# Moving 12 modulation chunks of a diffusion trunk's first stage from TensorE to VectorE

## The chip, the cores and the metric

One Trainium2 chip, one of its cores. The time is the device time of one execution in microseconds (us): lower is better. Before: 2353.95 us, the median of 3 runs (2353.66 to 2355.96). The engines are called PE (TensorE, the matmuls), DVE (VectorE), ACT (ScalarE), POOL (GpSimd) and SP (SyncE, whose queue issues the loads).

## The reference: what is computed

One step of a two-layer trunk (width D = 2048) over 128 context tokens `xp` and 128 latent tokens `xs`, all in fp32. Each layer is an attention half and an MLP half, and each half is scaled, shifted and gated by six vectors of 2048 that are made from a conditioning vector: `c_ctx` for the context tokens, `c` for the latent ones.

```python
def modulation(cvec, w_ada_l, b_ada_l):
    m = jax.nn.silu(cvec) @ w_ada_l + b_ada_l
    return jnp.split(m[:, None, :], N_MOD, axis=-1)
...
sh_a, sc_a, gt_a, sh_m, sc_m, gt_m = modulation(c, w_ada[l], b_ada[l])
h = rms_norm(xs, g_pre_a) * (1.0 + sc_a) + sh_a
...
o = mix_latent(h, ctx, w_in[l], w_out[l], na_rpb[l], gqa_q_g[l], gqa_k_g[l], ...)
xs = xs + gt_a * rms_norm(o, g_post_a)
h = rms_norm(xs, g_pre_m) * (1.0 + sc_m) + sh_m
xs = xs + gt_m * rms_norm(squared_relu_mlp(h, w_up[l], w_down[l]), g_post_m)
```

The context tokens go the same way with `c_ctx`. The attention has three kinds of heads side by side, one with a learned bias `na_rpb` by relative position, and small parameters for each layer (`qg`, `kg`, `dg`, `lam`). `w_ada` (2048 x 12288 for each layer) is as much work to load as the other weights, but is multiplied by two vectors only.

## The kernel before, in words

Every weight is read from HBM once, in chunks of 1 MB (128 x 2048 fp32) into one of `NRAW` = 5 buffers `raw`. The list `items` holds the order of the work, built by hand for each stage, and `issue` (L988) sends the loads on SP's queue in the order of that list, a new one when a buffer is released. There are four kinds of items.

- *Trunk chunk* ("t"). It is taken in two halves. For each, ACT rounds `raw` to `wh` (L1001) and DVE makes the remainder `wl` = `raw` - `wh` (L1002); 3 buffers of each, so that the split runs up to two halves ahead. PE multiplies a chunk by 24 products of 128 x 512 (L349 to L351: high by high, high by low, low by high) or, in the MLP's first product, by 48 of 128 x 256 (L384 to L386). In the first stage the sums of a segment are added up by DVE in `stg` (L782).
- *Modulation chunk on PE* ("ada", `ada_mm`, L140). 8 matmul records against the silu of the two conditioning vectors in `sT`. After four chunks (a block: 512 of the 2048 outputs of one of the six vectors) ACT copies the sum to `pt` (L144), PE transposes it (L111), DVE reduces it (L157), and `mod_fin` (L174, L175, L177) or `gate_fin` finishes it.
- *Modulation chunk on DVE* ("dv", `dv_mul`, L195). The transposed weights `w_adaT` are multiplied by `sB`, the silu of a conditioning vector copied to all partitions, and summed along the row: one multiply of 128 x 2048 into `junk` for the context tokens, and one into `raw` itself for the latent tokens, behind which the buffer is released. Up to two such chunks wait in `dvq`; each half of a trunk chunk moves the queue by half a step, or by a whole one while two wait. `sB` comes from two 1 MB loads and two activations (`load_sb`, L185, L187).
- *Call*: code that runs at that point of the list, such as `layer_consts` (L675 to L700). It loads `qg`, `kg`, `dg` into `bcs`, then `lam`, then the bias table `rpb` into `cv`; writes the table to DRAM (`rpbz`, L692); and reads it back in four pieces with other strides (`biasB`, L698). SP waits for the landing of each of the last three before it sends the next. DVE's and ACT's part is L676 to L686 and L700.

`weave` spreads modulation chunks among trunk chunks. The list says in which order the program is written; a scheduler with a cost model then sets each engine's order, so an operation can stand somewhat before or behind its place in the list.

The first stage of layer 0 is the start, a first quarter of the features (t0 to t7 and the modulation that it needs), feature quarters 2 to 4 (`f` = 1 to 3, t8 to t31), the rest of the input projection (`c2`, t32 to t35), and the output projection (`rest`, t36 to t51). Attention runs in between. Modulation is in blocks: M_A (shift and scale of the attention half), G_A (its gate), M_M and G_M (the same for the MLP). Of this stage 80 chunks are on PE, 8 in the first quarter as half-width pieces. The stage ends with `after_attn`: `use` runs four more modulation chunks that were loaded early into the `XT` buffers, `drain_dv` and `drain_fast` finish what is pending, `residual` (L309 to L321) makes the new `x`, with four L314 for each kind of token, and `make_xt` (L248 to L267) normalises and transposes it for the MLP. In the MLP's list of layer 0, 64 dv chunks are woven among the trunk chunks.

## Time and profile before

| what | value |
| --- | --- |
| median of 3 runs | 2353.95 us |
| the profiled execution, own time | 2356.2 us |
| its span in the profile | 2354.4 us |
| granted clock of PE, mean | 0.99 |
| PE busy | 2281.3 us (97%) |
| DVE busy | 1613.0 us (69%) |
| ACT busy | 1101.0 us (47%) |
| chain that ended last | PE 87%, DVE 5%, DMA 3%, ACT 2%, issue 2% |

The profiled execution is 2.25 us above the median, and its span leaves out 1.8 us around it. The shares are means over stages with different limits: the first stage (to about 490 us) carries attention and most of the modulation on PE, the MLP of layer 0 carries dv chunks on DVE.

### The profile page before, as it was taken

Reading aid. Unit: us, or ns where it says so; the run is one execution under the profiler, and the core shown is the slowest. Engines: PE = TensorE matmul, PEld = TensorE weight load, DVE = VectorE, ACT = ScalarE, POOL = GpSimd, SP = SyncE. Lnnn points to the kernel's source line nnn. Section 1 sums busy time; section 2 is a strip of 40 time slices with the busy share of each in tenths; the row PEclk is TensorE's granted clock in tenths of the full one; section 3 lists DMA queues with packets and bytes.
Section 4 is the critical chain, followed back from the end, with each engine's and each line's share of the span. In section 5 each row is a group of like instructions: output and inputs, shape, how many; then the busy total and the mean of one; then the engine's idle time right before and its main releaser. Section 6 shows DMA issues by size and latency. Waiting matters only on the chain.

```text
span 2354.4 us, 33079 instructions
## 1 busy us (share of the span) xinstructions
PE 2281.3 (97%) x13480; PEld 1905.2 (81%) x13480; DVE 1613.0 (69%) x2028; ACT 1101.0 (47%) x1525; POOL 25.6 (1%) x30
## 2 busy tenths in 40 slices
PE   6999999989999999999998999999999999999998
PEld 3567666669889889889867777877989988988986
DVE  2566755479888998999767787647666566565545
ACT  4334444464444445435445455546444444543543
POOL 0000000000000000000000000000000000000000
PEclk9999999999999999999999999999999999999999
DMA  8888787878877778777845766675666566565552
GB/s 323 305 328 336 274 321 302 332 249 303 308 269 292 292 293 294 279 286 286 337 179 197 270 223 233 226 268 200 228 217 219 211 221 222 201 219 212 191 183 90
DMA packets 92496, 601.35 MB, mean 255 GB/s; under 512 B 13752, under 2 KB 16184, under 8 KB 21432
## 3 DMA queue, kind: packets, MB, share of 16 engines
q1 hardware_dynamic: 91624, 598.64, 68.9%
q8 instruction: 105, 1.72, 0.3%
q10 hardware_dynamic: 720, 0.61, 0.1%
q14 instruction: 47, 0.39, 0.0%
HBM read 591.61 MB, written 7.60 MB: 255 GB/s over the span
## 4 chain that ended last, share of the span: by engine, by line
PE 87%; DVE 5%; DMA 3%; ACT 2%; issue 2%; POOL 1%; SPq 0%; ACTq 0%; POOLq 0%; DVEq 0%
PE acc L349 16%; PE acc L350 16%; PE acc L351 16%; PE acc L386 10%; PE acc L385 10%; PE acc L384 10%; PE ada L140 3%; PE m L111 2%; DVE wl L1002 2%; DMA raw<-w_adaT_in 2%; PE m L472 1%; POOL st L108 1%; PE m L223 1%; DVE raw L195 1%; DVE junk L195 0%
## 5 line engine op out<-in xcount | busy, mean ns | idle before, releaser
L1001 ACT ACTIVATE wh<-raw 128x1024 fp32r<-128x1024 f32 x720 | 759.0, 1059 | 924.0 <-PE acc L351 542.9
L1002 DVE TENSOR_TENSOR wl<-raw,wh 128x1024 fp32r<-128x1024 f32 x720 | 875.0, 1223 | 430.3 <-ACT wh L1001 427.7
L386 PE MATMUL acc<-XT,wl 128*128 128x256 f32 x2048 | 580.9, 284 | 1.6 <-DVE wl L1002 1.4
L385 PE MATMUL acc<-XT,wh 128*128 128x256 f32 x2048 | 580.1, 283 | 0.3 <-DVE XT L267 0.3
L384 PE MATMUL acc<-XT,wh 128*128 128x256 f32 x2048 | 577.6, 282 | 2.8 <-ACT XT L266 2.8
L349 PE MATMUL acc<-wh,big 128*128 128x512 f32 x1280 | 502.2, 395 | 0.0
L350 PE MATMUL acc<-wl,big 128*128 128x512 f32 x1280 | 499.9, 391 | 1.7 <-DVE wl L1002 1.7
L351 PE MATMUL acc<-wh,big 128*128 128x512 f32 x1280 | 498.2, 390 | 0.0
L384 PEld LDWEIGHTS acc<-XT,wh 128*128 128x128 f32 x2048 | 388.1, 190 | 4.3 <-ACT XT L266 3.5
L386 PEld LDWEIGHTS acc<-XT,wl 128*128 128x128 f32 x2048 | 387.5, 189 | 2.8 <-DVE wl L1002 2.6
L385 PEld LDWEIGHTS acc<-XT,wh 128*128 128x128 f32 x2048 | 386.8, 189 | 1.1 <-DVE XT L267 0.8
L349 PEld LDWEIGHTS acc<-wh,big 128*128 128x128 f32 x1280 | 239.9, 188 | 63.9 <-issue 11.0
L350 PEld LDWEIGHTS acc<-wl,big 128*128 128x128 f32 x1280 | 240.4, 188 | 52.0 <-DVE wl L1002 3.5
L351 PEld LDWEIGHTS acc<-wh,big 128*128 128x128 f32 x1280 | 240.3, 188 | 50.3
L349 PE MATMUL acc<-wh,XT 128*128 128x512 f32 x576 | 231.0, 411 | 6.8 <-ACT wh L1001 4.0
L195 DVE SCALAR_TENSOR_TENSOR junk<-raw,sB 128x2048 fp8e5<-128x2048 f32 x92 | 210.5, 2288 | 33.1 <-DMA raw<-w_adaT_in 32.7
L350 PE MATMUL acc<-wl,XT 128*128 128x512 f32 x576 | 230.4, 400 | 2.4 <-DVE wl L1002 2.3
L351 PE MATMUL acc<-wh,XT 128*128 128x512 f32 x576 | 228.4, 397 | 0.0
L195 DVE SCALAR_TENSOR_TENSOR raw<-raw,sB 128x2048 f32<-128x2048 f32 x92 | 210.3, 2286 | 0.0
L349 PEld LDWEIGHTS acc<-wh,XT 128*128 128x128 f32 x576 | 108.6, 190 | 48.7 <-ACT wh L1001 11.3
L350 PEld LDWEIGHTS acc<-wl,XT 128*128 128x128 f32 x576 | 109.3, 190 | 32.3 <-DVE wl L1002 7.5
L351 PEld LDWEIGHTS acc<-wh,XT 128*128 128x128 f32 x576 | 109.0, 189 | 24.6 <-issue 0.2
(134 smaller groups left out, 1235.6 us busy)
## 6 DMA issues: line engine op xcount, KB each, us to landing
raw<-w_up_in SPq DMA_DIRECT2D x128, 1024.0 KB, 5.2
raw<-w_down_in SPq DMA_DIRECT2D x128, 1024.0 KB, 5.0
raw<-w_adaT_in SPq DMA_DIRECT2D x92, 1024.0 KB, 4.9
raw<-w_ada_in SPq DMA_DIRECT2D x80, 1024.0 KB, 6.3
raw<-w_in_in SPq DMA_DIRECT2D x72, 1024.0 KB, 5.6
raw<-w_out_in SPq DMA_DIRECT2D x32, 1024.0 KB, 4.9
XT<-w_ada_in SPq DMA_DIRECT2D x12, 1024.0 KB, 7.6
raw<-w_ada_in SPq DMA_DIRECT2D x16, 512.0 KB, 5.1
```

The source lines that it names most:

```text
L108: pool.tensor_tensor(out, out, hf[:, 0:width], ALU.pow)
L111: pe.transpose(out, in_, ident)
L140: pe.matmul(pa[32 * g:32 * g + 32, 0:w], sT[:, 4 * kq + g, :], raw[:, g * w:(g + 1) * w], start=(kq == 0), stop=(kq == 3), tile_position=( ...
L195: dve.scalar_tensor_tensor(o, raw, 1.0, sB[v], ALU.mult, ALU.mult, accum_out=a[:, j, v:v + 1], saturate=None if v else False)
L349: pe.matmul(a, xh, wh[:, c], start=first, stop=False)
L350: pe.matmul(a, xh, wl[:, c], start=False, stop=False)
L351: pe.matmul(a, xl, wh[:, c], start=False, stop=last)
L384: pe.matmul(a, wh[:, c], xh, start=first, stop=False)
L385: pe.matmul(a, wh[:, c], xl, start=False, stop=False)
L386: pe.matmul(a, wl[:, c], xh, start=False, stop=last)
L1001: act.activation(wh, r, AF.Copy)
L1002: dve.tensor_tensor(wl, r, wh.bitcast(F32), ALU.subtract)
```

## The change

Three blocks of layer 0, twelve chunks, go from "ada" to "dv": G_A[0], G_A[1] and the last of M_M. Three of them are woven into the second feature quarter, three into the third, two into the fourth, and four are handed to the output projection's list. The fill on PE shrinks from 48 to 36 chunks: 8 in the fourth quarter as before, 4 instead of 8 in `c2`, and the rest in the output projection. `load_sb` moves from the MLP's list to just before `layer_consts`. The MLP's 64 dv chunks are spread over 116 entries of its list instead of 115, from one earlier on.

```diff
--- before.py
+++ after.py
@@ -34,8 +34,8 @@
 G_A, G_M = [(2, b) for b in range(4)], [(5, b) for b in range(4)]
 M_A = [(i, f) for f in range(4) for i in range(2)]
 M_M = [(3 + i, f) for f in range(4) for i in range(2)]
-DV_BLOCKS = [G_M, M_A + M_M[:4] + G_A[:3] + G_M]
-PE_BLOCKS = [M_A[2:] + G_A + M_M, M_M[4:] + G_A[3:]]
+DV_BLOCKS = [G_A[:2] + M_M[7:] + G_M, M_A + M_M[:4] + G_A[:3] + G_M]
+PE_BLOCKS = [M_A[2:] + G_A[2:] + M_M[:7], M_M[4:] + G_A[3:]]

@@ -812,7 +812,7 @@
         c2 = tchunks(wi, 32, 4, g2, k4)
         if l == 0:
             items.insert(0, ("call", startup))
-            fill, dv = ada_items(0, G_A + M_M), []
+            fill, dv = ada_items(0, G_A[2:] + M_M[:7]), dv_items(0, G_A[:2] + M_M[7:])
             h0 = lambda h: [("ada", I["w_ada0"][sec, h, kq], (0, sec, 0, kq, h)) for sec in range(2) for kq in range(4)]
             items.extend(h0(0)[:2])
             call(pre_norm_first)
@@ -826,19 +826,22 @@
             items.extend(a1[:2] + m[3:4] + a1[2:4] + m[4:5] + a1[4:6] + m[5:6] + a1[6:] + m[6:7])
             xt(1)
             items.extend(m[7:])
+            call(load_sb)
             for f in range(1, 4):
                 ch = [c for cg in cG for c in cg[2 * f:2 * f + 2]]
                 if f == 1:
                     call(lambda l=l: layer_consts(l))
                 if f < 3:
-                    weave(ch[:5], ada_items(0, M_A[2 * f + 2:2 * f + 4]))
+                    weave(ch[:5], ada_items(0, M_A[2 * f + 2:2 * f + 4]), dv[:3])
+                    dv = dv[3:]
                     items.append(ch[5])
                     xt(f + 1)
                     items.extend(ch[6:])
                 else:
-                    weave(ch, fill[:8])
-            weave(c2, fill[8:16])
-            rest, fill = [], fill[16:]
+                    weave(ch, fill[:8], dv[:2])
+                    dv = dv[2:]
+            weave(c2, fill[8:12])
+            rest, fill = [], fill[12:]
         else:
             for f in range(4):
                 call(lambda f=f: make_xt(1, 0, f))
@@ -877,11 +880,14 @@
             rest += tchunks(I["w_out"][l], 8 * nh, 8, Group(2, KT, o_lhs(), wout_done(nh)), ko, need)
             if nh == 0:
                 rest.append(("call", load))
-        cut = 0 if l == 0 else 40
+        cut = 20 if l == 0 else 40
         nf = (len(fill) - TAIL) * cut // len(rest) // 2 * 2
-        if cut:
+        if l == 0:
+            weave(rest[:cut], fill[:nf])
+            weave(rest[cut:], fill[nf:], dv, tail=TAIL)
+        else:
             weave(rest[:cut], fill[:nf], dv)
-        weave(rest[cut:], fill[nf:], tail=TAIL)
+            weave(rest[cut:], fill[nf:], tail=TAIL)

         def after_attn(S=S, l=l, use=use):
             use()
@@ -941,14 +947,13 @@
             if q == 3 and l + 1 < L:
                 rest.insert(-8, ("call", load))
         if l + 1 < L:
-            rest.insert(1, ("call", load_sb))
             g, m = dv_items(0, G_M), dv_items(1, M_A + M_M[:4])
             dv = [x for i in range(16) for x in m[3 * i:3 * i + 3] + g[i:i + 1]]
-            weave(rest[:4], [])
-            weave(rest[4:119], [], dv)
+            weave(rest[:2], [])
+            weave(rest[2:118], [], dv)
             call(lambda: drain_dv())
             call(lambda l=l: layer_consts(l + 1))
-            items.extend(rest[119:])
+            items.extend(rest[118:])
         else:
             weave(rest[:2], [])
             weave(rest[2:100], [], dv_items(1, G_M))
```

Lines behind the edits have numbers five higher in the new kernel (L988 is L993, L1002 is L1007).

SP's queue at the constants of layer 0, in the order in which it sends the loads. Before:

```order
L675 DMA bcs<-qg_in 128x128
L675 DMA bcs<-kg_in 128x128
L675 DMA bcs<-dg_in 128x128
L678 DMA cv<-lam_in 128x256
L690 DMA cv<-rpb_in 12x31
L988 DMA raw<-w_in_in 128x2048
L692 DMA rpbz<-cv 768x1x127
L988 DMA raw<-w_in_in 128x2048
L698 DMA biasB<-rpbz 64x4x64 x4
L988 DMA raw<-w_ada_in 128x2048 x2
```

And with the change:

```order
L185 DMA sB_89<-crow_in 128x2048
L185 DMA sB_90<-crow_in 128x2048
L675 DMA bcs<-qg_in 128x128
L675 DMA bcs<-kg_in 128x128
L675 DMA bcs<-dg_in 128x128
L678 DMA cv<-lam_in 128x256
L690 DMA cv<-rpb_in 12x31
L993 DMA raw<-w_ada_in 128x2048
L692 DMA rpbz<-cv 768x1x127
L993 DMA raw<-w_adaT_in 128x2048
L698 DMA biasB<-rpbz 64x4x64 x4
L993 DMA raw<-w_in_in 128x2048 x2
```

The two loads of `sB` stand ahead of the constants; the two weight loads among the constants are modulation now, where they were trunk weights (`w_in`), and the next trunk weights stand behind `biasB`.

DVE in the same place. Before:

```order
L681 TENSOR_TENSOR cv<-cv 128x128
L683 TENSOR_REDUCE st_773<-cv 128x2
L782 TENSOR_TENSOR stg<-stg,acc 128x512
L685 TENSOR_TENSOR lam<-st_773 128x1
L686 TENSOR_SCALAR lam<-lam 128x1
L157 TENSOR_REDUCE st_88<-m 128x8
L177 TENSOR_TENSOR mod_1_76<-st_88,baT 128x4 x2
L1002 TENSOR_TENSOR wl<-raw,wh 128x1024 x4
L700 TENSOR_TENSOR biasB<-biasB,cs 128x512
```

And with the change:

```order
L681 TENSOR_TENSOR cv<-cv 128x128
L683 TENSOR_REDUCE st_777<-cv 128x2
L685 TENSOR_TENSOR lam<-st_777 128x1
L686 TENSOR_SCALAR lam<-lam 128x1
L157 TENSOR_REDUCE st_88<-m 128x8
L177 TENSOR_TENSOR mod_1_76<-st_88,baT 128x4 x2
L195 SCALAR_TENSOR_TENSOR junk,aacc<-raw,sB_89 128x2048
L195 SCALAR_TENSOR_TENSOR raw,aacc<-raw,sB_90 128x2048
L700 TENSOR_TENSOR biasB<-biasB,cs 128x512
L1007 TENSOR_TENSOR wl<-raw,wh 128x1024 x4
```

A pair of multiplies and the addition on the bias (L700, which waits for `biasB`) stand ahead of the four `wl`, where the four `wl` stood ahead of L700.

DVE at the end of the stage, in `residual`. Before:

```order
L248 TENSOR_SCALAR big<-stg,st_3680 128x512
L314 SCALAR_TENSOR_TENSOR stg<-stg,st_3684 128x512 x4
L321 TENSOR_REDUCE st_3697<-st_3688 128x1
L107 TENSOR_SCALAR st_3697<-st_3697 128x1
L157 TENSOR_REDUCE st_88<-m 128x8
```

And with the change:

```order
L314 SCALAR_TENSOR_TENSOR stg<-stg,st_3652 128x512
L195 SCALAR_TENSOR_TENSOR junk,aacc<-raw,sB_89 128x2048
L157 TENSOR_REDUCE st_88<-m 128x8
L195 SCALAR_TENSOR_TENSOR raw,aacc<-raw,sB_90 128x2048
L195 SCALAR_TENSOR_TENSOR junk,aacc<-raw,sB_89 128x2048
L174 SCALAR_TENSOR_TENSOR mod_2_77<-st_88,baT 128x4 x2
L195 SCALAR_TENSOR_TENSOR raw,aacc<-raw,sB_90 128x2048
L175 TENSOR_TENSOR mod_2_77<-mod_2_77,ngT 128x4 x2
L195 SCALAR_TENSOR_TENSOR junk,aacc<-raw,sB_89 128x2048
L157 TENSOR_REDUCE st_88<-m 128x8
L195 SCALAR_TENSOR_TENSOR raw,aacc<-raw,sB_90 128x2048
L195 SCALAR_TENSOR_TENSOR junk,aacc<-raw,sB_89 128x2048
```

The four L314 of the latent tokens, which followed one another, have eight multiplies among them (the eighth, the pair to the last row, follows); these belong to the four dv chunks that were handed to the output projection's list.

## Rows read from the trace of the kernel before

**Rows 1.** The page: span, and busy time of each engine.

```profile
span 2354.4 us, 33079 instructions
...
PE 2281.3 (97%) x13480; PEld 1905.2 (81%) x13480; DVE 1613.0 (69%) x2028; ACT 1101.0 (47%) x1525; POOL 25.6 (1%) x30
```

**Rows 2.** Windows of 50 us: length, busy PE, PEld, DVE, ACT, POOL; clock, DMA share, GB/s.

```profile
100.00:150.00 50.00, 47.50 (x230) 31.61 (x229) 27.17 (x46) 17.45 (x23) 0.00 (x0) 1.00 0.85 314
...
200.00:250.00 50.00, 49.81 (x242) 37.41 (x241) 34.22 (x59) 27.66 (x34) 2.66 (x2) 1.00 0.85 324
...
950.00:1000.00 50.00, 50.00 (x230) 41.28 (x228) 47.50 (x53) 21.27 (x24) 0.00 (x0) 1.00 0.77 284
```

**Rows 3.** PE's timeline at the stage's end: start, duration, operation, idle before and its releaser.

```profile
467.61 0.39 PE L351 MATMUL acc<-wh,big 128*128 128x512 f32 x1
...
480.47 1.93 PE L140 MATMUL ada<-XT,sT 128*32 128x512 f32 x8 [4.80 <-ACT pt L144]
...
488.65 1.04 PE L111 MATMUL m<-cs,big 128*128 128x128 f32 x8
491.90 0.50 PE L384 MATMUL acc<-XT,wh 128*128 128x256 f32 x2 [2.21 <-ACT XT L266]
```

**Rows 4.** The chain that ended last: start, us, what.

```profile
81.20 1.90 PE ada L140 x16
...
101.61 6.68 DMA cv<-rpb_in
...
109.32 11.43 DMA raw<-w_in_in
```

**Rows 5.** PE's timeline at the constants of layer 0.

```profile
115.63 0.66 PE L111 MATMUL m<-cs,pt 128*128 128x128 f32 x4 [0.72 <-ACT pt L144]
116.58 1.20 PE L349 MATMUL acc<-wh,XT 128*128 128x512 f32 x4 [0.29 <-ACT wh L1001]
```

**Rows 6.** Groups of DVE instructions by line and form: busy, mean ns | idle before.

```profile
L1002 DVE TENSOR_TENSOR wl<-raw,wh 128x1024 fp32r<-128x1024 f32 x720 | 875.0, 1223 | 430.3 <-ACT wh L1001 427.7 <-PE m L223 1.7
...
L195 DVE SCALAR_TENSOR_TENSOR junk<-raw,sB 128x2048 fp8e5<-128x2048 f32 x92 | 210.5, 2288 | 33.1 <-DMA raw<-w_adaT_in 32.7
L195 DVE SCALAR_TENSOR_TENSOR raw<-raw,sB 128x2048 f32<-128x2048 f32 x92 | 210.3, 2286 | 0.0
```

**Rows 7.** SP's timeline: issues of the bias constants and of sB.

```profile
108.31 0.92 SPq L692 DMA_DIRECT2D rpbz<-cv  x1
...
116.31 2.65 SPq L698 DMA_DIRECT2D biasB<-rpbz  x4
...
208.76 0.53 SPq L185 DMA_DIRECT2D sB<-crow_in  x1
```

**Rows 8.** Windows around the constants and in the output projection, columns as in rows 2.

```profile
404.00:414.00 10.00, 10.00 (x41) 6.87 (x39) 5.43 (x7) 6.85 (x13) 0.00 (x0) 1.00 0.99 393
...
98.00:106.00 8.00, 8.00 (x33) 4.57 (x32) 4.41 (x6) 2.25 (x3) 0.00 (x0) 1.00 0.44 161
...
120.00:148.00 28.00, 26.70 (x135) 18.44 (x134) 15.91 (x25) 11.88 (x16) 0.00 (x0) 1.00 1.01 412
```

**Rows 9.** DMA issues on the page: count, KB each, median us to landing.

```profile
raw<-w_in_in SPq DMA_DIRECT2D x72, 1024.0 KB, 5.6
```

**Rows 10.** Windows of 2 us at the stage's end, columns as in rows 2.

```profile
480.00:482.00 2.00, 1.53 (x8) 0.20 (x8) 0.00 (x0) 2.00 (x3) 0.00 (x0) 0.50 0.97 410
...
486.00:488.00 2.00, 1.38 (x16) 0.16 (x8) 0.22 (x1) 0.49 (x1) 0.00 (x0) 1.00 0.46 78
```

**Rows 11.** DVE's timeline at the stage's end: the latent tokens' L314.

```profile
474.61 2.74 DVE L314 SCALAR_TENSOR_TENSOR stg<-stg,st 128x512 f32<-128x512 f32 x4
```

**Rows 12.** ACT's timeline at the stage's end: the normalising copy.

```profile
479.21 0.72 ACT L250 ACTIVATE big<-stg,st 128x512 f32<-128x512 f32 x1 [1.10 <-POOL st L108]
```

## The prediction, as it was made before the run

> **What bounds the kernel now.** I read the page first, then the windows, the chain, and last the timelines of the two places where the change lands. The page shows TensorE (PE) busy 2281.3 of 2354.4 us and VectorE (DVE) 1613.0 [rows 1]: PE is the bound, DVE has room on average. The windows say where. Among the first stage's chunks, at 100 to 150 us, PE is busy 47.5 of 50 and DVE 27.2; in the MLP, at 950 to 1000 us, where the "dv" chunks already run, PE is busy all 50 with DVE at 47.5 [rows 2]. So multiplies on DVE can be free, under two conditions that I check below: DVE must not hold back a `wl` that PE wants, and the extra loads must not hold back SP, which issues every load in one order. At the end of the stage neither the one nor the other kind of slack is needed: PE is through with its trunk at 468.0 (467.61 + 0.39) and the MLP's first matmul starts at 491.90, and in those 23.9 us PE has only modulation chunks and transposes while DVE and ACT make the residual [rows 3].
>
> **What is removed.** A pair of modulation chunks holds PE for 1.90 us when the chain goes through it [rows 4], so 0.95 us a chunk. The order shows 10 of the 12 ahead of the last trunk matmul: 6 raw chunks come behind it before, 4 after. 10 x 0.95 = 9.5, and two and a half blocks fewer to transpose, 0.66 each [rows 5], give 1.6: **-11 us**. The other two chunks lay inside the 23.9 us, and count there.
>
> **What is added on DVE.** 12 x 2 multiplies of 2.29 us [rows 6] are 55 us, 4.57 us a chunk, against 0.95 us taken from PE. They are cheap only where DVE idles anyway. I price four places.
>
> *The constants of layer 0 (about 100 to 132 us).* Before, SP sends the bias load `rpb`, waits for its landing (6.68 us, behind one 1 MB load), sends `rpbz` at 108.31, waits again, and sends the four `biasB` from 116.31 to 118.96; two weight loads slip between [rows 4, 7]. The one issued at 109.32 is on the chain with 11.43 us to its landing [rows 4]. Now 2 MB of `sB` and a modulation chunk stand ahead of `rpb`, and of the two loads that slip between, both are modulation, where before both were trunk weights. The trunk chunk that PE wants next (t10, first matmul at 116.58 before [rows 5]) is issued only behind `biasB`. Working: `rpb` lands later by what 2 MB needs; the queue moved 0.44 of its capacity at 98 to 106 us and 412 GB/s when full [rows 8], so 5.1 us if nothing of it fits in the idle share and about 4 with some of it hidden; `rpbz` at 112.3, `biasB` 8.0 us later at 120.3, sent in 2.65, the weight load at 123. It lands 5.6 us later at the median of its line [rows 9], 11.4 at the slowest of these; I take 8, since SP's stop leaves a queue of loads to catch up on, as at 120 to 148 us, where the DMA share is 1.01 [rows 8]. That is 131; the split of its first half takes ACT and DVE about a microsecond, so t10 begins near 132: a stall of **+15 us**. Bounds: `sB` wholly hidden and the landing in 5.6 us, together with PE's work of the moved chunks, give +5; `rpb` 6 us later with the slow landing +20. Behind such a stop the granted clock was 0.50 (its lower level, 1.2 GHz), after the 4.80 us that PE waited at the end of the stage, and 1.00 again by 486 us [rows 3, 10]: **+2 us**, being half of the 4 us or so in which work went at half speed (0 to 3).
>
> Beside it, the Trainium skill's page "DMA: Bandwidth & Descriptors", section "Queues, rings and completion order", says that on one DMA engine a later descriptor's completion promises the earlier ones' reads, not their writes; were that all, a 1.5 KB load need not stand behind all of `sB`, and this term would be near +11 and the sum +20. The row of 6.68 us speaks for a full wait behind the earlier load.
>
> *Feature quarters 2 to 4.* DVE goes in its written order. The order puts pairs of multiplies between the accumulations that end a segment (L782) and the next `wl`, at t12, t18 and t20. At t20 both follow the last L782: 4.57 + 1.22 for the next `wl`, against a pair of chunks (1.90) and the four first products that need no `wl` (1.20) on PE [rows 4, 5, 6]: 2.7 us. At t12 and t18 one multiply overlaps the wait for the accumulation: about 1 us each. **+5 us**; 0 if PE is late there for other reasons, 12 if at all three PE has only the pair (3 x 3.9).
>
> *The output projection.* The diff asks for four dv chunks there, but `rest` has 17 entries and `cut` is 20, so `rest[cut:]` is empty and the four (and two fill chunks) come behind the last trunk chunk. What does arrive here is layer 1's constants, whose loads and waits on SP moved from the MLP to just ahead of t46. DMA is at 0.99 there [rows 8], so a stop of SP of the kind at 101 to 119 costs something, though it meets five buffers: **+2 us** (0 to 6).
>
> *The end of the stage.* `drain_dv` now runs 8 multiplies between the first and the last L314 of the latent tokens, 8 x 2.29 = 18.3 us. Before, these L314 begin at 474.61, ACT scales the result at 479.21, done at 479.93, but PE transposes it only at 488.65, since the four held chunks and their transposes are ahead [rows 3, 11, 12]: 8.7 us of slack. 18.3 - 8.7 = 9.6, and the block's own sums and the clock behind the idle add about 1: the first MLP matmul comes 34.9 us after the trunk's last instead of 23.9, **+11 us**. Bounds: one pair earlier in DVE's few gaps, +6; the last of the 4 MB late (10 us at 412 GB/s, as the loads wait for buffers), +14.
>
> *The rest.* The MLP's 64 dv chunks start one trunk chunk earlier, under a PE that is 100% busy [rows 2]: 0; if that cover were gone it would be one multiply, 2.3 us. The `sB` load leaves its place at 208.76 us, where PE was busy 49.81 of 50: 0 [rows 2, 7].
>
> **Sum:** -11 + 15 + 2 + 5 + 2 + 11 = +24 us. The profiled execution took 2356.2 us (span 2354.4), 2.25 above the median of 2353.95; set against the median, as both would shift alike, the forecast is **2378 us**. The low ends give -11 + 5 + 0 + 0 + 0 + 6 = 0, 2354; the high ends -11 + 20 + 3 + 12 + 6 + 14 = +44, 2398.
>
> **Rivals.** *The multiplies and loads hide (faster).* Every `wl` and weight load keeps its lead, and at the end of the stage the scheduled DVE work fits in the slack. Then all 12 chunks and three blocks' transposes count: 12 x 0.95 + 2.0 = 13.4, 2341 us. For it: the MLP, where DVE at 95% delays nothing [rows 2]. It decides as soon as the two places (constants and end) together add less than 13 us. Against: at the constants SP already stops and the chain goes through it [rows 4], and 18.3 us do not fit into 8.7. The Trainium skill's "Perfetto Trace Analysis", section "Identifying Performance Opportunities", sends one to the most-contended engine and would expect this side; by it the time is 2341. Chance 0.07.
>
> *Only the end of the stage costs.* `sB` fits into the 56% of the DMA that idle at 98 to 106 [rows 8] and t10 is there in time, the quarters cost 3: -11 + 11 + 3 = +3, 2357 us. For it: that idle share. Against: SP's two waits in a row stand in either case. Chance 0.09.
>
> *The stream starves in the whole stage.* A multiply chunk keeps its buffer for 4.57 us where PE's kept it 0.95, and there are five. If each of the eight in the quarters delays a weight load by half of the 3.6 us: +14, so +38, 2392 us. For it: DMA at 0.85 of its capacity at 100 to 150 us and PE without reserve there [rows 2]. Against: DVE is idle 23 of those 50 us, so a chunk is mostly taken up at once. Chance 0.12.
>
> **How the numbers follow.** The forecast has 0.72. A measurement tells about 0.2% from no change, 4.7 us, so "same" is 2349 to 2359. Faster: the first rival, 0.07. Same: the second, 0.09, and the lowest part of the forecast's own range, 0.02: 0.11. Slower: the rest, 0.82. The range takes the ends of the sum, drawn in by 2 at the top, where all bounds would have to fall together: 2354 to 2396; outside lie the first rival, half of the third's upper tail and little else.
>
> **What would show it.** Right: a PE idle of some 15 us between 115 and 135 us that ends on a weight load issued behind `biasB`; waits of 1 to 3 us on `wl` at t12, t18, t20; about 35 us between the trunk's last L351 and the first L384, with eight L195 inside; L140 down by 12 chunks, DVE up by 55 us; the MLP as long as before. Wrong: t10 starting by 120 us, or the first L384 within 28 us of the last L351, either of which takes off 10 us; or a stall where I priced nothing, above all in the MLP's first chunks, whose loads wait for the buffers of the four late dv chunks.

## The result and the profile after

The changed kernel takes 2384.72 us (median of 4 runs, 2382.53 to 2388.14) against 2354.37 us for the kernel before, a ratio of 1.0131 with a 95% interval of 1.0118 to 1.0143: 30 us slower. The forecast was 2378 us, the range 2354 to 2396. One of the five executions of e6 below took 6806.88 us at a mean granted clock of 0.33; its time below is the median of the other four.

The page of the changed kernel, the lines that answer to [rows 1]:

```profile
span 2383.4 us, 32890 instructions
...
PE 2280.1 (96%) x13372; PEld 1907.8 (80%) x13372; DVE 1665.6 (70%) x2073; ACT 1098.3 (46%) x1520; POOL 28.5 (1%) x30
```

PE has 108 records fewer and DVE is busy 52.6 us longer, so the chunks did move. Yet PE's busy time is the same within 1.2 us, where the moved work should have taken 13.4 off. A matmul at the lower clock is busy for longer (a 128x512 product 0.63 us at 132.04 us, 0.39 at 136.03), and PE is busy for 41.1 us at the lower level now, for 27.2 before; that makes some 7 of the 12 us that are missing.

PE's timeline shows where the span grew. First one row of the kernel before (one of the attention's last steps, ahead of the output projection's main part), as a mark that both kernels have:

```profile
390.04 0.82 PE L111 MATMUL m<-cs,big 128*128 128x128 f32 x4 [1.10 <-DVE big L488]
```

Then PE's timeline of the changed kernel (start, duration, operation, idle before and its releaser):

```profile
117.05 1.07 PE L140 MATMUL ada<-raw,sT 128*32 128x512 f32 x8 [2.32 <-DMA raw<-w_ada_in]
120.37 1.12 PE L111 MATMUL m<-cs,pt 128*128 128x128 f32 x4 [2.25 <-ACT pt L144]
130.19 1.22 PE L349 MATMUL acc<-wh,XT 128*128 128x512 f32 x2 [8.71 <-ACT wh L1006]
...
149.64 0.50 PE L350 MATMUL acc<-wl,XT 128*128 128x512 f32 x1 [1.59 <-DVE wl L1007]
...
194.86 1.20 PE L349 MATMUL acc<-wh,XT 128*128 128x512 f32 x4 [1.62 <-ACT wh L1006]
...
214.62 0.50 PE L350 MATMUL acc<-wl,XT 128*128 128x512 f32 x1 [2.51 <-DVE wl L1007]
...
409.58 0.63 PE L111 MATMUL m<-cs,big 128*128 128x128 f32 x3 [1.09 <-DVE big L488]
...
489.78 0.39 PE L351 MATMUL acc<-wh,big 128*128 128x512 f32 x1
...
519.33 1.97 PE L111 MATMUL m<-cs,big 128*128 128x128 f32 x8 [18.22 <-ACT big L250]
521.99 0.80 PE L384 MATMUL acc<-XT,wh 128*128 128x256 f32 x2 [0.70 <-ACT XT L266]
```

From these marks and those of [rows 3, 5] the 29.0 us of the two spans (2383.4 - 2354.4) divide as follows. The last column is the sum of the forecast's terms for the stretch, with the removed chunks set where PE's records (L140, L111) have them fewer: six chunks and two blocks up to the mark, -7.0; four chunks from there to the last L351, -3.8 (half a block less than the -11 took).

| stretch | before, us | after, us | difference | forecast |
| --- | --- | --- | --- | --- |
| start to t10's first matmul | 116.58 | 130.19 | +13.6 | +15 |
| t10 to the mark in attention | 273.46 | 279.39 | +5.9 | 2 + 5 - 7.0 = 0 |
| the mark to the trunk's last L351 | 77.96 | 80.59 | +2.6 | 2 - 3.8 = -1.8 |
| last L351 to the first L384 | 23.90 | 31.82 | +7.9 | +11 |
| MLP of layer 0 to the end | 1862.5 | 1861.4 | -1.1 | 0 |

The chain that ended last goes through the constants of layer 0 again, now by other loads than in [rows 4]:

```profile
103.43 9.79 DMA cv<-rpb_in
113.23 7.90 DMA rpbz<-cv
...
123.84 5.15 DMA raw<-w_in_in
```

The 1.5 KB of `rpb` land 9.79 us after their issue, with `sB`'s 2 MB ahead of them, where they took 6.68 without it. The windows that matter, with the columns of [rows 2]:

```profile
120.00:136.00 16.00, 6.89 (x18) 4.85 (x19) 9.39 (x13) 3.61 (x5) 0.00 (x0) 0.53 0.90 342
...
415.00:420.00 5.00, 5.00 (x28) 4.21 (x26) 3.17 (x9) 2.04 (x8) 0.00 (x0) 0.99 0.06 19
...
445.00:450.00 5.00, 3.16 (x17) 1.31 (x11) 2.29 (x7) 3.43 (x4) 0.00 (x0) 0.92 0.85 321
450.00:455.00 5.00, 5.00 (x18) 3.92 (x18) 2.10 (x3) 1.06 (x1) 0.00 (x0) 0.74 0.92 378
...
500.00:519.00 19.00, 1.09 (x8) 0.85 (x8) 19.00 (x38) 6.43 (x12) 0.62 (x1) 0.60 0.83 301
519.00:528.00 9.00, 7.98 (x37) 7.58 (x38) 7.86 (x15) 6.14 (x15) 0.00 (x0) 0.52 0.42 127
```

The reader sees three holes. At 120 to 136 us PE has 6.89 us of work and a clock of 0.53. At 415 to 420 us the DMA share is 0.06 while PE still works, and at 445 to 455 us PE has idle time and a lower clock. At 500 to 519 us DVE is busy all the time and PE next to never, and the MLP then begins at 0.52. In SP's timeline the second one lies at layer 1's constants:

```profile
409.40 0.45 SPq L447 DMA_DIRECT2D ck<-c_gqa_k_in  x1
423.63 0.33 SPq L678 DMA_DIRECT2D cv<-lam_in  x1
...
431.77 3.12 SPq L993 DMA_DIRECT2D raw<-w_out_in  x2
```

From 409.85 to 423.63 SP sends nothing: its next load goes into a `cv` buffer, of the kind that attention's `c_na_v` is loaded into; which of its readers SP waited for, the trace doesn't name. No weight load passes until 431.77. Whether the constants make this pause is tried in e3. DVE's timeline names the third:

```profile
494.94 0.75 DVE L314 SCALAR_TENSOR_TENSOR stg<-stg,st 128x512 f32<-128x512 f32 x1
495.61 2.29 DVE L195 SCALAR_TENSOR_TENSOR junk<-raw,sB 128x2048 fp8e5<-128x2048 f32 x1
...
515.60 0.75 DVE L314 SCALAR_TENSOR_TENSOR stg<-stg,st 128x512 f32<-128x512 f32 x1
```

Eight multiplies stand between the first and the last L314 of the latent tokens, 21.4 us from start to end instead of the 2.74 of [rows 11].

### The profile page after: what moved, and what is told of

It reads as the page before. It is cut to its first block, busy times and chain, and to the rows that moved or that the text cites. A ratio compares the mean times of both kernels' runs of the same rounds, so it can differ in the third digit from the quotient of the medians.

```text
span 2383.4 us, 32890 instructions
## 1 busy us (share of the span) xinstructions
PE 2280.1 (96%) x13372; PEld 1907.8 (80%) x13372; DVE 1665.6 (70%) x2073; ACT 1098.3 (46%) x1520; POOL 28.5 (1%) x30
## 4 chain that ended last, share of the span: by engine, by line
PE 88%; DVE 4%; DMA 3%; ACT 2%; issue 1%; POOL 1%; SPq 0%; ACTq 0%; POOLq 0%; DVEq 0%
PE acc L350 17%; PE acc L349 17%; PE acc L351 17%; PE acc L386 10%; PE acc L385 10%; PE acc L384 10%; PE ada L140 3%; PE m L111 2%; DVE wl L1007 1%; DVE junk L195 1%; DMA raw<-w_adaT_in 1%; PE m L472 1%; POOL st L108 1%; DVE raw L195 1%; DMA raw<-w_in_in 1%
## 5 line engine op out<-in xcount | busy, mean ns | idle before, releaser
L1006 ACT ACTIVATE wh<-raw 128x1024 fp32r<-128x1024 f32 x720 | 759.7, 1059 | 963.0 <-PE acc L351 574.5
L1007 DVE TENSOR_TENSOR wl<-raw,wh 128x1024 fp32r<-128x1024 f32 x720 | 875.8, 1223 | 433.5 <-ACT wh L1006 430.8
L384 PE MATMUL acc<-XT,wh 128*128 128x256 f32 x2048 | 578.6, 283 | 1.0 <-ACT XT L266 1.0
L351 PE MATMUL acc<-wh,big 128*128 128x512 f32 x1280 | 499.1, 391 | 0.0
L384 PEld LDWEIGHTS acc<-XT,wh 128*128 128x128 f32 x2048 | 388.7, 190 | 2.7 <-ACT XT L266 1.8
L351 PEld LDWEIGHTS acc<-wh,big 128*128 128x128 f32 x1280 | 240.8, 188 | 50.2
L195 DVE SCALAR_TENSOR_TENSOR junk<-raw,sB 128x2048 fp8e5<-128x2048 f32 x104 | 237.9, 2287 | 33.7 <-DMA raw<-w_adaT_in 33.6
L195 DVE SCALAR_TENSOR_TENSOR raw<-raw,sB 128x2048 f32<-128x2048 f32 x104 | 237.7, 2286 | 0.1
L351 PE MATMUL acc<-wh,XT 128*128 128x512 f32 x576 | 230.1, 401 | 0.0
L350 PEld LDWEIGHTS acc<-wl,XT 128*128 128x128 f32 x576 | 110.3, 192 | 39.6 <-DVE wl L1007 13.6
L351 PEld LDWEIGHTS acc<-wh,XT 128*128 128x128 f32 x576 | 110.4, 192 | 24.5
```

What stands on the lines that cost most here:

```text
L195: dve.scalar_tensor_tensor(o, raw, 1.0, sB[v], ALU.mult, ALU.mult, accum_out=a[:, j, v:v + 1], saturate=None if v else False)
L350: pe.matmul(a, xh, wl[:, c], start=False, stop=False)
L351: pe.matmul(a, xl, wh[:, c], start=False, stop=last)
L384: pe.matmul(a, wh[:, c], xh, start=first, stop=False)
L1006: act.activation(wh, r, AF.Copy)
L1007: dve.tensor_tensor(wl, r, wh.bitcast(F32), ALU.subtract)
```

## The experiments

Two theories were tried against each other: that the time is lost at three places where something queues in the wrong order (the constants, the output projection, the residual), each of which can be mended; or that a multiply of 2.29 us and its megabyte cost about as much wherever they are put in this stage. Where a kernel has twelve dv chunks, they are the same twelve. Some edits move line numbers by one or two (L993, L1006 and L1007 of the change are L995, L1008 and L1009 in e2, e3 and e8).

**e1: the four late chunks woven into the output projection.**

```diff
-        cut = 20 if l == 0 else 40
+        cut = 10 if l == 0 else 40
-            weave(rest[:cut], fill[:nf])
-            weave(rest[cut:], fill[nf:], dv, tail=TAIL)
+            weave(rest[:cut], fill[:nf], dv)
+            weave(rest[cut:], fill[nf:], tail=TAIL)
```

> The four late dv chunks are spread over the first ten entries of the output projection, so no multiply stands among the L314 any more. Theory (the end of the stage costs what DVE does there): the gap from the trunk's last L351 to the first L384 falls from 31.8 us to about 24, and the time from 2384.7 to about 2377. Rival (the multiplies cost their 18 us wherever they are put, since wl comes late behind them): the gap falls, but the output projection is longer by as much, and the time stays within 3 us of 2384.7.

Measured: 2372.33 us, 1.0073 (1.0058 to 1.0088) of before, so 12.4 less than the change. PE's timeline:

```profile
397.71 0.48 PE L111 MATMUL m<-cs,tmp 128*128 128x128 f32 x1 [3.17 <-DVE tmp L664]
...
488.34 0.39 PE L351 MATMUL acc<-wh,big 128*128 128x512 f32 x1
...
510.43 0.50 PE L384 MATMUL acc<-XT,wh 128*128 128x256 f32 x2 [2.20 <-ACT XT L266]
```

The gap is 510.43 - 488.73 = 21.7 us instead of 31.8: the end of the stage is shown to cost about 10 us. The trunk's last L351 does not come later for it (488.73 instead of 490.17), against the rival. The MLP, which no longer begins at half clock, takes 2368.9 - 510.43 = 1858.5 instead of 1861.4; that this is the clock's doing is not shown, for e8's MLP begins at half clock too, at 522.20, and takes 1859.0. The multiplies are not free in their new place, though: attention waits 3.17 us for an L664 (1.06 at that step in the changed kernel).

**e2 and e3: the constants' loads on POOL's queue**, of layer 0 alone (e2, shown) and of layer 1 alone (e3, with `l == 1`). In both the copy of the bias table goes in two pieces, also for the layer that stays on SP, and `dynamic_dma_scratch_size` is 1664 instead of 1024.

```diff
     def layer_consts(l):
+        q = nc.gpsimd if l == 0 else nc.sync
...
-            nc.sync.dma_start(bcs[:, i, :], I[nm][l:l + 1, :].to_broadcast([P, P]))
+            q.dma_start(bcs[:, i, :], I[nm][l:l + 1, :].to_broadcast([P, P]))
...
-        nc.sync.dma_start(sc, rz.unsqueeze(1).to_broadcast([12, 64, 127]))
+        for i in range(0, 12, 6):
+            q.dma_start(sc[i:i + 6], rz[i:i + 6].unsqueeze(1).to_broadcast([6, 64, 127]))
```

> The loads of layer 0's constants go on POOL's queue instead of SP's (the bias table's copy to DRAM in two pieces); all twelve dv chunks and the sB load stay. Theory (SP's two stops in a row, behind 2 MB more, hold back t10's weights): the idle of 8.7 us ahead of t10 and the lower clock behind it go; 12 to 15 us less, about 2371. Rival (the stream lacks bandwidth for sB and the dv chunks): t10 waits for its weights all the same, less than 4 us gained, 2381 or more.

Measured: 2394.09 us, 1.0163 (1.0148 to 1.0178), slower by 9.4 than the change. On its own queue the load was free to go at once, and the scheduler sent it at the very start, among the first weights. PE's timeline, at the start, at t10 and in the MLP:

```profile
42.69 2.25 PE L140 MATMUL ada<-raw,sT 128*32 128x256 f32 x10 [5.18 <-DMA raw<-w_ada_in]
...
132.09 0.79 PE L350 MATMUL acc<-wl,XT 128*128 128x512 f32 x1 [4.69 <-DVE wl L1009]
...
548.72 0.39 PE L384 MATMUL acc<-XT,wh 128*128 128x256 f32 x1 [2.96 <-ACT wh L1008]
551.85 0.58 PE L386 MATMUL acc<-XT,wl 128*128 128x256 f32 x1 [2.39 <-DVE wl L1009]
```

The start costs 8.9 us: t9's first matmul comes at 116.78 instead of 107.89. By t24's (239.35, in the change 239.47) all of it is made up. So in its place the theory holds for 9 us of its 12 to 15, and at t10, with SP free of the constants, the wait that is left is for `wl`, 4.69 us, behind DVE's multiplies. At the MLP's first matmul e2 is even 4.1 us ahead of the change (517.90). What makes the kernel slower lies behind that: its MLP takes 1872.8 us instead of 1861.4, with new waits of 2.96 and 2.39 us. Their cause was not looked for, so the total says nothing of the constants.

> The same for layer 1's constants alone, whose loads stop SP from 409.8 to 423.6 us in the output projection of the changed kernel. Theory (that stop starves the output projection): DMA no longer idles there, the waits at 447 to 450 us and the lower clock behind them go, 5 to 9 us less, about 2378. Rival (the output projection is longer for the multiplies' or the gates' sake): no change, 2384 to 2386.

Measured: 2384.38 us, 1.0122 (1.0107 to 1.0137), no change in all. The stretch from the mark (413.40 here) to the last L351 (488.65) takes 75.3 us instead of 80.6, and the window that was the worst is full. But DMA still pauses, and so does SP, though it has no constants to send. Windows, then SP's timeline:

```profile
420.00:425.00 5.00, 5.00 (x28) 3.20 (x27) 2.01 (x6) 1.27 (x5) 0.00 (x0) 1.00 0.00 0
...
445.00:450.00 5.00, 5.00 (x28) 2.77 (x27) 1.91 (x2) 1.68 (x3) 0.35 (x1) 1.00 0.87 314
```

```profile
413.09 0.42 SPq L447 DMA_DIRECT2D ck<-c_gqa_k_in  x1
430.94 0.33 SPq L995 DMA_DIRECT2D raw<-w_out_in  x1
```

From 413.51 to 430.94 SP sends nothing. Between weight loads the pause is 17.9 us (413.03 to 430.94), where it is 22.9 in the change (408.88 to 431.77). So the constants lengthen the pause and don't make it: the theory is right in the waits at 447 to 450 us, which are gone, and wrong in that DMA would no longer idle. The 5.3 us went elsewhere: t10 began at 132.98 instead of 130.19 (the copy in two pieces, on SP, lengthens the constants of layer 0), and the gap at the end was 34.3 instead of 31.8.

**e4: only `load_sb` moved, no chunk on DVE.**

```diff
+            call(load_sb)
             for f in range(1, 4):
...
-            rest.insert(1, ("call", load_sb))
```

> The kernel before with one edit: load_sb stands ahead of layer 0's constants, no chunk goes to DVE. Theory: rpb lands about 4 us later behind the 2 MB, but the two loads that slip between the constants are still trunk weights, so t10 waits 4 to 6 us only; the layer-1 constants' loads move into the output projection here too and cost some more: 2359 to 2366. Rival (the 2 MB alone make the stall): t10 waits as in the changed kernel, 13 us, 2367 or more. Rival (idle DMA time takes the 2 MB): 2354.

Measured: 2361.69 us, 1.0027 (1.0015 to 1.0038), inside the theory's 2359 to 2366. t10:

```profile
119.74 0.79 PE L349 MATMUL acc<-wh,XT 128*128 128x512 f32 x1 [3.61 <-ACT wh L1001]
```

It starts 3.2 us later than in [rows 5], against 13.6 with the change. By t13's first matmul e4 is 5.9 us behind the kernel before (the change 15.9), by the MLP's first 9.0, and its MLP is 1.8 us shorter. So about a fifth of the changed kernel's loss is there before a single chunk has moved, and 2 MB alone don't make the hole at t10.

**e5: e1, with layer 0's constants at the fourth quarter.**

```diff
-                if f == 1:
+                if f == 3:
                     call(lambda l=l: layer_consts(l))
```

> As e1, and the call of layer 0's constants stands at the fourth feature quarter instead of the second; sB is loaded where it was. So rpb, rpbz and biasB no longer stand between sB and the weights of t10. Theory (SP's two stops make most of the stall, the 2 MB a third of it): t10 waits 2 to 5 us instead of 13, 8 to 11 us less than e1, about 2363; a part may come back where the stops are now. Rival (the 2 MB and the dv chunks starve t10): t10 waits 8 us or more all the same, 2369 or more.

Measured: 2373.84 us, 1.0069 (1.0051 to 1.0087): no gain over e1. The rival's number, but not by its mechanism:

```profile
121.18 0.96 PE L349 MATMUL acc<-wh,XT 128*128 128x512 f32 x3 [2.33 <-ACT wh L1006]
...
126.68 0.80 PE L350 MATMUL acc<-wl,XT 128*128 128x512 f32 x1 [4.54 <-DVE wl L1007]
```

The weights do arrive earlier (2.33 us of wait), as the theory had it. Then PE waits 4.54 us for `wl`, which stands behind four multiplies in a row on DVE; and four more waits of 1 to 2 us come up between 262 and 327 us, behind the constants' new place. Part of the gain is real: from t9's first matmul to t24's e5 takes 124.1 us and e1 131.5. It is lost again at the new place: at t27's first matmul e5 is 5.2 us ahead of e1 (252.63 against 257.81), at t28's 0.7 behind (266.05 against 265.36). The stop of SP had hidden a part of the wait for DVE.

**e6: eight chunks, all in the output projection.**

```diff
-DV_BLOCKS = [G_M, ...
+DV_BLOCKS = [M_M[6:] + G_M, ...
...
+            call(load_sb)
             weave(c2, fill[8:16])
...
-        cut = 0 if l == 0 else 40
+        cut = 11 if l == 0 else 40
```

> The kernel before with the last two blocks of M_M (8 chunks) on DVE, all spread over the first eleven entries of the output projection; sB's load stands ahead of the last part of the input projection, and the feature quarters are as before. Theory (a chunk saves 0.95 us of PE where neither SP nor wl is held up): 8 x 0.95 + 2 x 0.66 = 9 us less than before, about 2346. Rival (multiplies delay the output projection's evictions or the residual): 2355 or more.

Measured: 2367.47 us, 1.0043 (1.0017 to 1.0069). The rival is right. The quarters are undisturbed; attention, which runs in front of and among the output projection's chunks, is not. PE's timeline, then DVE's and POOL's ahead of it:

```profile
388.68 0.73 PE L111 MATMUL m<-cs,tmp 128*128 128x128 f32 x2 [7.66 <-DVE tmp L664]
```

```profile
382.69 2.29 DVE L195 SCALAR_TENSOR_TENSOR junk<-raw,sB 128x2048 fp8e5<-128x2048 f32 x1 [0.32 <-DMA raw<-w_adaT_in]
...
384.90 0.17 DVE L107 TENSOR_SCALAR st<-st 128x4 f32<-128x4 f32 x1
385.08 2.29 DVE L195 SCALAR_TENSOR_TENSOR raw<-raw,sB 128x2048 f32<-128x2048 f32 x1
...
388.27 1.13 DVE L664 SCALAR_TENSOR_TENSOR tmp<-m,st,bcs 128x128 f32<-128x128 f32 x4 [0.89 <-POOL st L108]
```

```profile
385.21 3.02 POOL L108 TENSOR_TENSOR st<-st,hf 128x4 f32<-128x4 f32 x1 [28.77 <-DVE st L107]
```

An attention head is a chain of short steps that goes back and forth between PE, ACT, DVE and POOL. Here L107 waits for the first multiply, and POOL's L108, which comes next, takes 3.02 us beside the second one. Of this form (128x4) it takes 1.02 in the kernel before:

```profile
240.10 1.02 POOL L108 TENSOR_TENSOR st<-st,hf 128x4 f32<-128x4 f32 x1 [222.70 <-DVE st L107]
```

**e7: the kernel before, with layer 0's constants at the fourth quarter** (e5's edit).

> The kernel before with the call of layer 0's constants at the fourth feature quarter, nothing else. Theory (before, the stop of SP is covered by the five buffers, PE waits about 1 us there): within 3 us of before, 2352 to 2356. Rival (the stop costs PE more than its one wait shows, by the catch-up of the loads behind it): 2350 or less.

Measured: 2363.28 us, 1.0029 (1.0018 to 1.004): slower by 7, which neither side had. The constants stand among attention's steps now, L157 behind L434 and the constants' L700 on DVE, and PE waits twice:

```profile
241.04 0.66 PE L111 MATMUL m<-cs,pt 128*128 128x128 f32 x4 [3.85 <-ACT pt L144]
...
246.13 0.47 PE L111 MATMUL m<-cs,ck 128*128 128x128 f32 x1 [4.00 <-DVE st L157]
```

At their old place the constants' leaving gains 4.2 us (e7 is 1.9 us behind the kernel before at t9's first matmul and 2.4 ahead at t13's), more than the wait of 1 us that the theory had counted there. At the new place 10.6 us are lost: at t27's first matmul e7 is 1.8 us ahead, at t29's 8.8 behind. How much of the two waits in between is the constants' was not separated.

**e8: no dv chunk in the second quarter; four in the third and four in the fourth, `sB` loaded at the third.** The loads at the constants are those of the kernel before.

```diff
-            call(load_sb)
...
+                if f == 2:
+                    call(load_sb)
                 if f < 3:
-                    weave(ch[:5], ada_items(0, M_A[2 * f + 2:2 * f + 4]), dv[:3])
-                    dv = dv[3:]
+                    nd = 4 * (f - 1)
+                    weave(ch[:5], ada_items(0, M_A[2 * f + 2:2 * f + 4]), dv[:nd])
+                    dv = dv[nd:]
...
-                    weave(ch, fill[:8], dv[:2])
-                    dv = dv[2:]
+                    weave(ch, fill[:8], dv[:4])
+                    dv = dv[4:]
```

> The changed kernel with its first eight dv chunks four by four in the third and fourth quarters, none in the second, and sB loaded at the third; so the loads at layer 0's constants are those of the kernel before, and nothing else differs from the changed kernel. Theory (the 13 us and the lower clock behind them come of what stands among the constants): t10 starts as in the kernel before, 10 to 16 us less; four chunks in one quarter cost 2 to 5 us more there; about 2374. Rival (the eight multiplied chunks cost their DVE time wherever they are in the quarters): the idle only moves to the third quarter, 2381 or more.

Measured: 2381.77 us, 1.0115 (1.0098 to 1.0132), 3 less than the change, the rival's number. The hole at t10 is gone, and one of the same kind is in the third quarter.

```profile
180.29 1.65 PE L349 MATMUL acc<-wh,XT 128*128 128x512 f32 x3 [3.68 <-ACT wh L1008]
...
202.26 0.79 PE L350 MATMUL acc<-wl,XT 128*128 128x512 f32 x1 [3.72 <-DVE wl L1009]
```

SP's timeline shows a part of what makes it:

```profile
149.54 0.33 SPq L995 DMA_DIRECT2D raw<-w_adaT_in  x1
...
161.08 0.90 SPq L185 DMA_DIRECT2D sB<-crow_in  x2
```

The first dv chunk is loaded at 149.54, but `sB` is sent at 161.08 and its silu begins at 169.18, so the first multiply starts at 172.66 and the buffer comes free at 177.3: one of five buffers is held for 28 us, while 2 MB more are loaded. Then multiplies stand ahead of `wl`. The hole does not move whole, though: at t24's first matmul e8 is 9.8 us ahead of the change (229.68 against 239.47), and 2.7 at t36's, behind the fourth quarter, where it has four dv chunks instead of two.

**e9: e8 and e1 together.**

> e8 and e1 together: no dv chunk at the constants of layer 0, none among the L314. Theory (the two terms add): 2384.7 less what e8 gains and less the 12.4 of e1, about 2362, still over before since wl waits in the quarters and attention's steps behind multiplies (2.0 and 3.2 us in e1) remain. Rival (with both places mended the chunks pay): 2351 or less.

Measured: 2371.63 us, 1.0066 (1.0047 to 1.0084): over the theory's 2362, for e8 had gained 3 and not 10 (e9's four executions range from 2363.43 to 2373.14); and e1 alone is as good. The chunks don't pay with both places mended.

**e10: e9, with the last block of M_M back on PE** (eight chunks, in the third and fourth quarters).

> As e9, but the last block of M_M goes back to PE: eight dv chunks, all in the third and fourth quarters, none in the output projection or attention. Theory (a chunk on PE costs 0.95, the four multiplied ones in e9 cost attention about 3): within 4 us of e9. Rival (DVE is free in the output projection, and PE bound): 3.8 plus a block's transposes 0.7, 4 to 6 us more than e9.

Measured: 2367.34 us, 1.0054 (1.0039 to 1.0069), 4.3 less than e9, where the rival had 4 to 6 more. The two intervals overlap, and the edit starts from the change, so `cut` is 20 again, which moves the fill as well; so what is shown is that moving these four chunks to DVE gains nothing, not that it costs 4 us.

**e11: the kernel before, with four chunks behind attention, in entries 8 to 15 of the output projection**; `sB` loads where the kernel before has it.

```diff
+            n0, n1 = [(len(fill) - TAIL) * i // len(rest) // 2 * 2 for i in (7, 15)]
+            weave(rest[:7], fill[:n0])
+            weave(rest[7:15], fill[n0:n1], dv)
+            weave(rest[15:], fill[n1:], tail=TAIL)
```

> The kernel before with one block of M_M (4 chunks) on DVE, spread over entries 8 to 15 of the output projection, behind the work of attention; sB loads where the kernel before has it. Theory (a chunk pays only where DVE has neither wl for the quarters, nor attention's steps, nor the residual to serve): 4 x 0.95 + 0.66 = 4.5 us less than before, about 2350. Rival (the moved loads of layer 1's constants, or the order of the loads, cost as much): 2354 or more.

Measured: 2364.46 us, 1.0033 (1.0019 to 1.0048). The rival again. Two of the four pairs reach DVE in attention all the same, at 390 and 398 us, and PE waits for the step behind one of them:

```profile
402.71 2.03 PE L111 MATMUL m<-cs,big 128*128 128x128 f32 x8 [1.82 <-DVE big L488]
```

The rest of the 9 us lies in the output projection as well (layer 1's constants are loaded in it here too, from 402.70 us on), and was not separated further.

**e12: e9, with G_A[1] back on PE**, so that the third quarter still loads `sB` and has no dv chunk.

> e9 with G_A[1] back on PE: four dv chunks in the fourth quarter, four in the output projection, none in the third, where sB is still loaded. Theory (in e8 the idle of the third quarter came of a dv chunk that holds one of five buffers until sB is there, and of four pairs of multiplies ahead of wl): the waits of 3.7, 1.2 and 3.2 us at 174 to 205 us shrink to under 3 in all, 3.8 + 0.7 come back on PE, 3 to 6 us less than e9, about 2366. Rival (the 2 MB of sB starve that quarter): the waits stay, 2371 or more.

Measured: 2367.63 us, 1.0049 (1.003 to 1.0069), 4.0 less than e9, as the theory had it, though the intervals overlap. The third quarter shows it plainly: the first matmuls of t17 and of t24, in e8 and then in e12:

```profile
166.17 0.50 PE L349 MATMUL acc<-wh,XT 128*128 128x512 f32 x1
...
229.68 0.40 PE L349 MATMUL acc<-wh,XT 128*128 128x512 f32 x1
```

```profile
165.86 0.50 PE L349 MATMUL acc<-wh,XT 128*128 128x512 f32 x1
...
216.33 0.40 PE L349 MATMUL acc<-wh,XT 128*128 128x512 f32 x1
```

The seven chunks take 63.5 us with `sB` and the four dv chunks and 50.5 with `sB` alone; the kernel before takes 47.2 (165.51 to 212.66), the change, with three dv chunks and no load of `sB`, 56.3. So `sB` costs some 3 us there and the four chunks 13, of which the lower clock behind the waits is a part. Whether the held buffer or the multiplies ahead of `wl` cost more was not separated, as e12 takes away both. Of the 13 us only 4 are left in the total: four chunks are back on PE, and from t36's first matmul to the first L384 e12 takes 188.5 us where e9 takes 175.1.

**The second and third quarters side by side.** From t9's first matmul to t24's PE has the same trunk and modulation chunks in all these kernels. Traces that have the same edits there agree: the change 131.6 and e1 131.5, e8 121.5 and e9 121.6.

| kernel | what stands there | us | over before |
| --- | --- | --- | --- |
| before | the constants | 105.5 | |
| e7 | not even the constants | 101.8 | -3.7 |
| e12 | the constants, `sB` at the third quarter | 108.7 | +3.2 |
| e4 | `sB` and the constants | 111.5 | +6.1 |
| e8 | the constants, then `sB` and four dv chunks | 121.5 | +16.1 |
| e2 | `sB`, six dv chunks; the constants loaded on POOL's queue | 122.6 | +17.1 |
| e5 | `sB`, six dv chunks | 124.1 | +18.6 |
| the change | `sB`, the constants, six dv chunks | 131.6 | +26.1 |

Neither of the two theories holds alone. With the constants out of SP's way six dv chunks and `sB` still cost 17 to 19 us; with them in the way it is 7 to 9 more.

The totals, with the number of chunks on DVE in this stage:

| kernel | chunks on DVE | us over before |
| --- | --- | --- |
| e4, `sB` alone | 0 | 6.5 |
| e11, e6 | 4, 8 | 9, 12 |
| e12, e10 | 8 | 12, 13 |
| e9, e1 | 12 | 17, 17 |
| e8, the change | 12 | 28, 30 |

No version beat the kernel before: the interval of each lies above 1. That every further block costs some 4 us more is the trend of the medians; between neighbouring rows the intervals overlap.

## Why the prediction was right, and where it was not

**The sign and the size.** The forecast's +24 is four fifths of the measured +30, and the two largest terms are the two largest holes. That the sum came so close is in part luck: the quarters and the output projection cost 10.3 us more than their terms, and the constants, the end of the stage and the MLP 5.6 less.

**The constants of layer 0: size right, cause too narrow.** Expected were `rpbz` at 112.3, `biasB` at 120.3, the weight load at 123 and t10 near 132; they came at 113.23, 121.15, 123.84 and 130.19 (the weight load landed in 5.15 us, not 8). SP waits here twice, for `rpb` and for `rpbz`; the weights follow `biasB` at once. The sentence "`rpb` lands later by what 2 MB needs" holds: it lands at 113.22 instead of 108.29, 4.9 us later, where 2 MB at 412 GB/s make 5.1 and the working took 4. The +11 that the prediction worked out beside it from the Trainium skill's "DMA: Bandwidth & Descriptors" used half of what the section "Queues, rings and completion order" says: a later descriptor may finish its write before an earlier one, but the semaphore's increment lands only after every earlier write of that DMA engine. SP waits for the semaphore, and the trace agrees with the second half: `rpb` lands after both loads of `sB`, whose activations begin at 107.16 and 109.70.

But the term was put down to SP's stops alone. Of the 13.3 us that PE idles between t9 and t10, 8.71 end on t10's weights; 2.32 end on a modulation load sent at 104.35, behind `sB`, and 2.25 on ACT's copy `pt`, which stands behind the constants' L684 as that stands behind a pair of multiplies on DVE. And e5 shows that without them PE waits 4.54 us for `wl` at the same spot, and e8 that with the chunks in another quarter the hole goes with them. The stop of SP, the buffer held by the first dv chunk (loaded at 88.41, free at 119.06), and the multiplies ahead of `wl` stood behind one another, and the first hid a part of the others. The rival that a dv chunk's held buffer starves the stream was given 0.12; its mechanism is seen (e8's 28 us), though its share was not separated and its 2392 us was not reached.

**The lower clock.** +2 us was taken. PE worked at 0.53 in the mean of 120 to 136 us, and t10's first matmuls came at a pitch of 0.43 us where 0.23 is usual, for 5 us: t10 took 8.16 us instead of 6.16, just the term. Further such stretches, at 197 to 200, 412 to 415, 449 to 453 and, in the MLP, up to 528 us, were not in the sum.

**Feature quarters: mis-sized.** The waits at t12, t18 and t20 were priced at 1, 1 and 2.7 us, and are 1.59, 1.62 (for `wh`) and 2.51: 5.7 against 5. But the quarters cost more than their waits. From t11's first matmul to t24's the change takes 101.1 us and the kernel before 89.9: +11.2, close to the bound of 12, and no chunk is taken from PE there. Of the rest the lower clock at 197 to 200 us is a part, and 1.1 us of transposes of the gate (L223), which comes earlier now; the remainder was not separated.

**The output projection: mis-sized.** "+2 us (0 to 6)" was written for layer 1's constants. With the 3.8 us of removed chunks the stretch should have been 1.8 us shorter, and was 2.6 longer: the term is 6.4, just over its bound. e3 shows that most of it, 5.3 us, goes when the constants are loaded from POOL. That SP stops there at all is mostly not their doing, as 17.9 us of the pause stay; what makes these was not separated.

**The end of the stage.** +11 was forecast, +7.9 came: the working took the first L314 of the latent tokens at 6.6 us behind the last L351, as before, and it came 4.8 behind (494.94 - 490.17). e1, whose gap is 21.7 us, shows that all of it, and the MLP's start at half clock, is the doing of the four late chunks. That the four are not in the output projection at all, because `rest` has 17 entries, was read right from the code.

**The savings.** -11 us was credited, and where chunks leave PE and hardly a multiply stands in their place it can be seen: from t28's first matmul to t41's six chunks and a block are gone, 6.4 us by the prices, and the change falls from 26.8 us behind the kernel before to 20.0. In the total the chunks that left PE were outweighed. The rival that all multiplies hide (2341 us), which the Trainium skill's "Perfetto Trace Analysis", section "Identifying Performance Opportunities", would lead one to by its most-contended engine, failed on both of its conditions; PE was the busiest engine before and after, at 97 and 96%, and what was taken from it came back as waits and lower clock.

## What to carry to other kernels

Work that is moved to an engine with idle time on average is paid for by whoever stands behind it in that engine's order: ask, for each place, which short step the next engine waits for (here `wl`, attention's L107, the residual's L314), and whether the moved operation, 2.29 us in one piece, can stand ahead of it. A chunk that waits for a second operand holds its stream buffer until that operand is there; loading the operand first would avoid it, which no run here tried. When a wait is removed and nothing is gained in all (e2, e5, e8), set the same trunk chunk of both traces side by side: the gain may be there, and lost again at another place.

## What the runs showed that was not expected

A short POOL step lasts longer beside a long DVE one. With no long DVE step beside it, L108 of 128x4 takes 1.01 to 1.02 us in the kernel before. It takes 3.02 in e6 and 2.96 in e1 (at 373.71 us), both beside an L195 that had begun 0.13 and 0.19 us ahead of it. Of 128x8 it takes 1.64 before, and 3.62 in the changed kernel, beside the L195 at 276.13; the kernel before has one such case itself, 3.55 at 1354.26. Beside a `wl` of 1.22 us L108 of 128x4 takes 1.92 (the changed kernel, 268.56). POOL's spans are rough, but the step that waits for it, L664 in e6, comes late by as much. The Trainium skill's "Trainium Architecture — The Big Picture", section "What this means for kernel authors", says that of the engines' ways into SBUF only the port pair of DVE and GpSimd is shared, as an exclusive lock; the rows agree, L108 being longer by 2.0 us where the L195 still had 2.2 to run, and by 0.9 where the `wl` had 1.05. So in e6 a pair of multiplies delays attention's chain twice, once in DVE's order and once on POOL.

A move of one load or of one call in the program shifts unrelated loads: in e4, where `load_sb` alone was moved, layer 1's `lam` is sent at 416.09 us, in the output projection, instead of 488.05, and in e7, where one call was moved, `sB` is sent at 494.29 instead of 208.76. PE's granted clock fell to its lower level, 1.2 GHz, at 118 us, among the waits of 2.32, 2.25 and 8.71 us, and at 504 us, in the wait of 18.22. It rose again some 5 us behind t10's first matmul and 6 us behind the MLP's, so that each hole was paid for a second time behind it.
